# Batch normalisation with ReLU on one core: the first store split into two of one row per partition, and ScalarE's order fixed

**Chip, cores, metric.** One core of one Trainium2 chip. The metric is device time in microseconds (us); the kernel before takes 84.19 us (median of 3 runs, 84.05 to 84.41). The span that a profile shows is about 1.9 us shorter than the time of the same run (82.3 against 84.21).

## The reference

```python
# x: (32, 128, 32, 32) float32; gamma, beta, running_mean, running_var: (128,)
normalized = (x - running_mean[None, :, None, None]) / np.sqrt(running_var[None, :, None, None] + eps)
scaled = normalized * gamma[None, :, None, None] + beta[None, :, None, None]
return np.maximum(scaled, 0).astype(np.float32)
```

16.78 MB are read and 16.78 MB written, with one activation (ReLU of scale times x plus bias) between.

## The kernel before

x is seen as two tiles of 128 partitions with 16 rows of 1024 floats each; a row is one image of one channel, 4 KB, and a partition's 16 rows lie next to each other in HBM. The loads come in six pieces, the stores follow the same pieces.

```python
PIECES = (((0, 2), (2, 4), (4, 8), (8, 16)), ((0, 8), (8, 16)))
# ...
    for t in range(T):
        for a, b in PIECES[t]:
            xt = data.tile([P, b - a, HW], F32, name=f"x{t}_{a}")
            nc.sync.dma_start(out=xt, in_=xr[t, :, a:b, :])        # load queue (q1)
            tiles.append((t, a, b, xt))
# ... scale_t and bias_t are made from four small parameter loads on ScalarE's queue ...
    for t, a, b, xt in tiles:
        for j in range(a, b):
            nc.scalar.activation(out=xt[:, j - a, :], in_=xt[:, j - a, :], func=ACTF.Relu,
                                 bias=bias_t[:, j : j + 1], scale=scale_t[:, j : j + 1])
        nc.scalar.dma_start(out=outr[t, :, a:b, :], in_=xt)        # store queue (q10)
```

A scheduler may move a store behind activations of the next piece, and it did. Each of these transfers runs on all 16 DMA engines; what one partition has in a transfer is one packet, so an engine gets 8 packets of each: 8, 8, 16, 32, 32 and 32 KB long.

Of the kernel before, what the change touches and what calls it, by code (L numbers as in the profile page):

```python
# [1 line left out]

# [4 lines left out]


F32 = mybir.dt.float32
ACTF = mybir.ActivationFunctionType  # L10



J = 16

PIECES = (((0, 2), (2, 4), (4, 8), (8, 16)), ((0, 8), (8, 16)))


@with_exitstack
def kernel(  # L20
    ctx: ExitStack,
    tc: tile.TileContext,
    x: bass.AP,
    gamma: bass.AP,
    beta: bass.AP,
    running_mean: bass.AP,
    running_var: bass.AP,
    eps: bass.AP,
    out: bass.AP,
):  # L30
    nc = tc.nc
    B, C, H, W = x.shape
    HW = H * W
    P = nc.NUM_PARTITIONS
    assert C % J == 0 and P % (C // J) == 0 and (B * C) % (P * J) == 0
    Q = C // J
    T = B * C // (P * J)

    xr = x.rearrange("b c h w -> (b c) (h w)").rearrange("(t p j) w -> t p j w", p=P, j=J)
    outr = out.rearrange("b c h w -> (b c) (h w)").rearrange("(t p j) w -> t p j w", p=P, j=J)  # L40

    data = ctx.enter_context(tc.tile_pool(name="data", bufs=1))
    params = ctx.enter_context(tc.tile_pool(name="params", bufs=1))
    psum = ctx.enter_context(tc.tile_pool(name="psum", bufs=1, space=bass.MemoryType.PSUM))

    tiles = []
# [3 lines that stand above are left out]
            nc.sync.dma_start(out=xt, in_=xr[t, :, a:b, :])  # L50
            tiles.append((t, a, b, xt))



    raw = params.tile([Q, 4, J], F32, name="raw")
    for k, src in enumerate((running_var, gamma, running_mean, beta)):
        nc.scalar.dma_start(out=raw[:, k, :], in_=src.rearrange("(q j) -> q j", j=J))  # L57
    eps_t = params.tile([P, 1], F32, name="eps_t")
    nc.vector.memset(eps_t, float(eps))  # L59
    rep = params.tile([Q, P // Q, Q], F32, name="rep")  # L60
    nc.gpsimd.memset(rep, 1.0)  # L61
    nc.gpsimd.affine_select(  # L62
        out=rep,
        in_=rep,
        compare_op=mybir.AluOpType.is_equal,
        fill=0.0,
        base=0,
        pattern=[[0, P // Q], [-1, Q]],
        channel_multiplier=1,
    )  # L70
    cols = psum.tile([P, 4, J], F32, name="cols")
    nc.tensor.matmul(  # L72
        cols.rearrange("p k j -> p (k j)"),
        rep.rearrange("q r s -> q (r s)"),
        raw.rearrange("q k j -> q (k j)"),
        start=True,
        stop=True,
    )
    std_t = params.tile([P, J], F32, name="std_t")
    nc.scalar.activation(out=std_t, in_=cols[:, 0, :], func=ACTF.Sqrt, bias=eps_t[:, 0:1], scale=1.0)  # L80
    rstd_t = params.tile([P, J], F32, name="rstd_t")
    nc.vector.reciprocal(out=rstd_t, in_=std_t)  # L82
    scale_t = params.tile([P, J], F32, name="scale_t")
    nc.vector.tensor_mul(out=scale_t, in0=cols[:, 1, :], in1=rstd_t)  # L84
    ms_t = params.tile([P, J], F32, name="ms_t")
    nc.vector.tensor_mul(out=ms_t, in0=cols[:, 2, :], in1=scale_t)  # L86
    bias_t = params.tile([P, J], F32, name="bias_t")
    nc.vector.tensor_sub(out=bias_t, in0=cols[:, 3, :], in1=ms_t)  # L88

    for t, a, b, xt in tiles:  # L90
        for j in range(a, b):
            nc.scalar.activation(  # L92
                out=xt[:, j - a, :],
                in_=xt[:, j - a, :],
                func=ACTF.Relu,
                bias=bias_t[:, j : j + 1],
                scale=scale_t[:, j : j + 1],
            )
        nc.scalar.dma_start(out=outr[t, :, a:b, :], in_=xt)


# [1 line left out]
_INS = ['x', 'gamma', 'beta', 'running_mean', 'running_var', 'eps']  # L103
_OUTS = [((32, 128, 32, 32), 'float32')]

_NUMBERS = {'eps': 1e-05}


# [26 lines left out]
```

## Time and profile before

| | kernel before |
|---|---|
| time, span | 84.19 us, 82.3 us |
| busy share of the 16 DMA engines, load + store queue | 48.6 + 47.5 = 96.1% |
| busy share of ScalarE | 46% |
| last load landed, last store issued, last store landed | 51.2, 60.4, 81.4 us |

The DMA engines are full from 2 to 80 us, so time is the sum of what their packets take. The lines are in the prediction.

For this document I use one more reading. The trace has start and duration of each DMA packet. An undisturbed packet takes 309 ns for 8 KB, 611 for 16 KB and 1213 for 32 KB, and most take just that. **Slow time** here means, for one run, the sum over all packets of duration minus the undisturbed duration of that size, divided by 16 engines. In the kernel before it is 0.44 us in the first 6 us (the first packets of all) and 0.56 us after that, nearly all in 32 KB load packets; from the moment that loads are over it is zero.

### The profile page before, as it was taken

The numbers are of one execution on the slowest core, as the hardware profiler recorded it, in microseconds if no ns is written. First come the engines' busy times: TensorE is split into PE (matmuls) and PEld (weight loads), VectorE is DVE, ScalarE is ACT, GpSimd is POOL, SyncE is SP. The second block draws the span as 40 slices with busy tenths as digits, with TensorE's granted clock in tenths as the row PEclk, the third lists the DMA queues.
The fourth block names the chain that finished last, engine by engine and source line by source line (L and its number), as shares of the span: only waits on it lengthen the run. The fifth ranks groups of instructions, "written<-read, shape, count | busy, mean of one in ns | idle before, by whom it ended". The sixth has DMA issues, their size and how long they took to land.

```text
span 82.3 us, 117 instructions
## 1 busy us (share of the span) xinstructions
PE 0.7 (1%) x2; PEld 0.5 (1%) x2; DVE 0.8 (1%) x5; ACT 38.2 (46%) x34; POOL 0.8 (1%) x6
## 2 busy tenths in 40 slices
PE   0003000000000000000000000000000000000000
PEld 0002000000000000000000000000000000000000
DVE  0000300000000000000000000000000000000000
ACT  0600599990009999509999401999930000000000
POOL 3000000000000000000000000000000000000000
DMA  2899999997998997997999898997998999799790
GB/s 36 315 431 486 398 486 398 462 430 319 462 526 351 462 430 327 582 430 319 446 510 446 382 382 374 518 478 303 494 494 366 414 510 446 319 510 478 303 494 0
DMA packets 1792, 33.56 MB, mean 408 GB/s; under 512 B 256, under 2 KB 256, under 8 KB 256
## 3 DMA queue, kind: packets, MB, share of 16 engines
q1 hardware_dynamic: 864, 16.78, 48.6%
q10 hardware_dynamic: 928, 16.78, 47.5%
HBM read 16.78 MB, written 16.78 MB: 408 GB/s over the span
## 4 chain that ended last, share of the span: by engine, by line
DMA 60%; ACT 10%; ACTq 1%; issue 1%
DMA x<-in_x_dram 53%; ACT x L92 10%; DMA raw<-in_beta_dram 6%; ACTq L57 1%
## 5 line engine op out<-in xcount | busy, mean ns | idle before, releaser
L92 ACT ACTIVATE x<-x,bias_t,scale_t 128x1024 f32<-128x1024 f32 x32 | 36.6, 1227 | 15.4 <-DMA x<-in_x_dram 14.4
L80 ACT ACT_TABLE_LOAD x1 | 1.3, 1283 | 2.7 <-issue 2.7
L80 ACT ACTIVATE std_t<-cols,eps_t 128x16 f32<-128x16 f32 x1 | 0.3, 273 | 4.1 <-PE cols L72 4.1
L72 PE MATMUL cols<-raw,rep 8*128 8x64 f32 x2 | 0.7, 428 | 7.4 <-DMA raw<-in_beta_dram 7.4
L72 PEld LDWEIGHTS cols<-raw,rep 8*128 8x128 f32 x2 | 0.5, 306 | 7.4 <-issue 7.4
L62 POOL TENSOR_SCALAR_AFFINE_SELECT rep<-rep 8x128 f32<-8x128 f32 x1 | 0.4, 393 | 0.1
L82 DVE RECIPROCAL rstd_t<-std_t 128x16 f32<-128x16 f32 x1 | 0.3, 253 | 7.5 <-ACT std_t L80 7.5
L61 POOL MEMSET rep<- 8x128 f32 x1 | 0.2, 194 | 0.3 <-POOLq L116 0.3
L84 DVE TENSOR_TENSOR scale_t<-cols,rstd_t 128x16 f32<-128x16 f32 x1 | 0.2, 175 | 0.1
L86 DVE TENSOR_TENSOR ms_t<-cols,scale_t 128x16 f32<-128x16 f32 x1 | 0.2, 175 | 0.0
L88 DVE TENSOR_TENSOR bias_t<-cols,ms_t 128x16 f32<-128x16 f32 x1 | 0.2, 175 | 0.0
L116 POOL MEMSET const-bfloat16-1.0<- 128x1 bf16 x1 | 0.1, 106 | 0.0
L116 POOL MEMSET const-uint8-127<- 128x1 uint8 x1 | 0.1, 106 | 0.0
L116 POOL MEMSET const-float32-0.0<- 128x1 f32 x1 | 0.1, 103 | 0.3 <-issue 0.3
L116 POOL MEMSET const-float32-1.0<- 128x1 f32 x1 | 0.1, 103 | 0.0
L59 DVE MEMSET eps_t<- 128x1 f32 x1 | 0.1, 59 | 0.9 <-PEq L116 0.9
## 6 DMA issues: line engine op xcount, KB each, us to landing
x<-in_x_dram SPq DMA_DIRECT2D x3, 4096.0 KB, 22.7
out_dram<-x ACTq DMA_DIRECT2D x3, 4096.0 KB, 21.0
x<-in_x_dram SPq DMA_DIRECT2D x2, 1024.0 KB, 6.0
x<-in_x_dram SPq DMA_DIRECT2D x1, 2048.0 KB, 11.4
out_dram<-x ACTq DMA_DIRECT2D x2, 1024.0 KB, 25.9
out_dram<-x ACTq DMA_DIRECT2D x1, 2048.0 KB
raw<-in_running_var_dram ACTq DMA_DIRECT2D x1, 0.5 KB
raw<-in_gamma_dram ACTq DMA_DIRECT2D x1, 0.5 KB
```

Of the source, the lines that this page charges most:

```text
L57: nc.scalar.dma_start(out=raw[:, k, :], in_=src.rearrange("(q j) -> q j", j=J))
L59: nc.vector.memset(eps_t, float(eps))
L61: nc.gpsimd.memset(rep, 1.0)
L62: nc.gpsimd.affine_select(out=rep, in_=rep, compare_op=mybir.AluOpType.is_equal, fill=0.0, base=0, pattern=[[0, P // Q], [-1, Q]], channel ...
L72: nc.tensor.matmul(cols.rearrange("p k j -> p (k j)"), rep.rearrange("q r s -> q (r s)"), raw.rearrange("q k j -> q (k j)"), start=True, s ...
L80: nc.scalar.activation(out=std_t, in_=cols[:, 0, :], func=ACTF.Sqrt, bias=eps_t[:, 0:1], scale=1.0)
L82: nc.vector.reciprocal(out=rstd_t, in_=std_t)
L84: nc.vector.tensor_mul(out=scale_t, in0=cols[:, 1, :], in1=rstd_t)
L86: nc.vector.tensor_mul(out=ms_t, in0=cols[:, 2, :], in1=scale_t)
L88: nc.vector.tensor_sub(out=bias_t, in0=cols[:, 3, :], in1=ms_t)
L92: nc.scalar.activation(out=xt[:, j - a, :], in_=xt[:, j - a, :], func=ACTF.Relu, bias=bias_t[:, j : j + 1], scale=scale_t[:, j : j + 1],)
L116: nc = _bacc.Bacc("TRN2", target_bir_lowering=False, num_devices=1)
```

## The change

The intent is to get the first bytes out earlier, and to have each store issued as soon as its data are ready.

```diff
+STORE_CUTS = {(0, 1)}
...
-    for t, a, b, xt in tiles:
-        for j in range(a, b):
-            nc.scalar.activation(...)
-        nc.scalar.dma_start(out=outr[t, :, a:b, :], in_=xt)
+    with tc.manual_schedule(engines={mybir.EngineType.Activation}):
+        for t, a, b, xt in tiles:
+            first = a
+            for j in range(a, b):
+                nc.scalar.activation(...)          # unchanged
+                if j + 1 == b or (t, j + 1) in STORE_CUTS:
+                    nc.scalar.dma_start(
+                        out=outr[t, :, first : j + 1, :], in_=xt[:, first - a : j + 1 - a, :]
+                    )
+                    first = j + 1
```

More of the change, by code (lines that the diff above doesn't have):

```diff
@@ L88 @@
     nc.vector.tensor_sub(out=bias_t, in0=cols[:, 3, :], in1=ms_t)
-    for t, a, b, xt in tiles:
-        for j in range(a, b):
-            nc.scalar.activation(
-                out=xt[:, j - a, :],
-                in_=xt[:, j - a, :],
-                func=ACTF.Relu,
-                bias=bias_t[:, j : j + 1],
-                scale=scale_t[:, j : j + 1],
-            )
-        nc.scalar.dma_start(out=outr[t, :, a:b, :], in_=xt)
+    with tc.manual_schedule(engines={mybir.EngineType.Activation}):
+        for t, a, b, xt in tiles:
+            first = a
+            for j in range(a, b):
+                nc.scalar.activation(
+                    out=xt[:, j - a, :],
+                    in_=xt[:, j - a, :],
+                    func=ACTF.Relu,
+                    bias=bias_t[:, j : j + 1],
+                    scale=scale_t[:, j : j + 1],
+                )
+                if j + 1 == b or (t, j + 1) in STORE_CUTS:
+                    nc.scalar.dma_start(
+                        out=outr[t, :, first : j + 1, :], in_=xt[:, first - a : j + 1 - a, :]
+                    )
+                    first = j + 1
 _INS = ['x', 'gamma', 'beta', 'running_mean', 'running_var', 'eps']
```

## The prediction

> **What bounds the kernel now.** I read the page first (busy shares, then the forty slices), next the chain of waits, the ACT timeline, and last the DMA view in narrow windows, because the first two already say that this is a transfer problem.
>
> ```profile
> PE 0.7 (1%) x2; PEld 0.5 (1%) x2; DVE 0.8 (1%) x5; ACT 38.2 (46%) x34; POOL 0.8 (1%) x6
> ...
> ACT  0600599990009999509999401999930000000000
> ...
> DMA  2899999997998997997999898997998999799790
> ...
> q1 hardware_dynamic: 864, 16.78, 48.6%
> q10 hardware_dynamic: 928, 16.78, 47.5%
> ```
>
> The two queues together keep the 16 DMA engines busy for 48.6 + 47.5 = 96.1% of the 82.3 us span, 79.1 us. The DMA row has an 8 or more almost everywhere from the second slice (2.1 us) to the 39th (80.2 us); the 7s are slice edges, since the engines run in step on packets longer than half a slice. ScalarE, the only busy compute engine, is at 46%, and its row is blank for the last quarter. So there is no stretch in the middle in which a DMA engine waits for a store to be issued. The gaps are at the two ends only: about 1.8 us before the first load packet and about 1 us after the last store data.
>
> The chain of waits names a different thing and must be read with care:
>
> ```profile
> 7.27 43.91 DMA x<-in_x_dram
> ...
> 52.35 8.01 ACT x L92 x7
> ```
>
> It runs over the last load (landed at 51.2), seven activations, and ends with the issue of the last store at 60.4 us; the remaining 21.9 us are the stores. But that last store did not start to move when it was issued: it queued. The order of work on ScalarE shows how early each store is handed over:
>
> ```profile
> 9.38 3.50 ACT L92 ACTIVATE x<-x,bias_t,scale_t 128x1024 f32<-128x1024 f32 x3 [1.03 <-DVE bias_t L88]
> 11.78 0.38 ACTq L99 DMA_DIRECT2D out_dram<-x  x1
> ...
> 37.00 1.24 ACT L92 ACTIVATE x<-x,bias_t,scale_t 128x1024 f32<-128x1024 f32 x1 [2.97 <-DMA x<-in_x_dram]
> 37.00 0.34 ACTq L99 DMA_DIRECT2D out_dram<-x  x1
> ...
> 51.21 1.24 ACT L92 ACTIVATE x<-x,bias_t,scale_t 128x1024 f32<-128x1024 f32 x1 [5.05 <-DMA x<-in_x_dram]
> 51.21 0.34 ACTq L99 DMA_DIRECT2D out_dram<-x  x1
> ```
>
> Each store comes out one activation late. The one at 37.00 had its data ready at 34.0, that at 51.21 at 46.2, and both sat behind an activation of the next piece, which waited for its load. The change removes these delays of 3 and 5 us. Whether that is worth anything depends on whether the store queue was empty meanwhile, and it was not: stores of 1 + 1 + 2 MiB (4.19 MB) are issued by 18.9 us, and the DMA view summed over windows from 0 to 50 us has q10 moving only about 3.6 MB. In the trace the third store's last packets go at about 51.5 us, when the fourth has waited since 37 and the fifth has just been issued. From there stores run back to back: each 4 MiB store takes 9.7 us, with last packets at about 61.2, 70.9 and 80.6 us.
>
> Three windows, each holding data packets of one size, give the price of a packet (0.75 MB over 91 is 8 KB, 1.28 over 78 is 16 KB, 2.52 over 77 is 32 KB):
>
> ```profile
> q1 hardware_dynamic: 91, 0.75, 97.7%
> ...
> q1 hardware_dynamic: 78, 1.28, 99.3%
> ...
> q10 hardware_dynamic: 77, 2.52, 97.3%
> ```
>
> They are 2.8 to 4.6, 8 to 11 and 54 to 60 us. Share times 16 engines times length over packets: 0.977 x 16 x 1.8 / 91 = 309 ns for 8 KB; 0.993 x 16 x 3 / 78 = 611 ns for 16 KB; 0.973 x 16 x 6 / 77 = 1213 ns for 32 KB. One packet is what one partition has in one transfer, so each engine gets 8 packets of every transfer. Sum for one engine, loads and stores alike: 32 of 8 KB (9.89) + 16 of 16 KB (9.78) + 48 of 32 KB (58.22) = 77.9 us. Add the start at 1.8 us and roughly a microsecond of slower packets (the first sixteen or so after the start, and some 32 KB ones of 1.25 to 1.5 us), and the end of data at 80.5 to 81.1 us is accounted for. That sum bounds the kernel.
>
> **What the Trainium skill says.** "Perfetto Trace Analysis", section DMA Optimizations, recommends splitting DMAs with a condition: "If DMA engines are generally idle, splitting DMAs into smaller sections may allow the overall task to complete sooner." The condition does not hold here, at 96.1% busy. "DMA: Bandwidth & Descriptors", section Queues, rings and completion order, says that each DMA engine goes round its queues packet by packet. The trace agrees if a packet is what its record calls one: between 40 and 49 us both queues moved 80 packets, q1 2.62 MB of 32 KB ones and q10 1.31 MB of 16 KB ones. The same page, section Why small descriptors are slow (HBM only), says that each packet has a small fixed overhead. The trace agrees: 611 - 2 x (611 - 309) = 7 ns does not scale with size.
>
> **The change part by part.**
>
> Split of the first store: 128 packets of 8 KB become 256 of 4 KB, thus 16 an engine in place of 8. By the fit, one of 4 KB takes 309 - 302/2 = 158 ns, an estimate, as no 4 KB packet is in this trace. 16 x 158 - 8 x 309 = 2528 - 2472 = 56 ns. One more completion packet at 9 ns (the trace's 4-byte packets) makes 65 ns. This is on the path, because the engines are the path: +0.07 us.
>
> One more issue on ScalarE's queue, and no activation overlapping an issue: a store costs 0.34 to 0.38 us there and now stands in front of the next activation. The first activation ends at 10.62, so the first half goes out near 10.65 in place of 11.78; the next activation starts near 11.0 in place of 10.53. By the fourth store ScalarE is 1 to 2 us behind (about 20 us, before 18.6), then waits for the load of the next piece anyway (24.9). Off the path: 0.
>
> Fixed order: the 4 MiB stores are issued when their data are ready. They join a queue with a backlog: 0 at the end.
>
> Earlier and smaller store packets change the interleaving. Beside loads of 32 KB, a round on one engine was 1213 + 309 ns for the first two stores (16 rounds). For the first it becomes 1213 + 158, with twice as many rounds. While the loads last, stores get less, so the loads finish earlier. They overlapped 8 + 8 store packets of 8 KB and 8 of 16 KB (9.8 us an engine); now they overlap 16 of 4 KB and about 8 of 8 KB (5.0 us). The last load should land about 4 to 5 us earlier, near 46 to 47 us, and the last store be issued near 56. What the loads gain the stores lose; bytes and engines are the same: 0.
>
> Semaphores: the program assigns its transfers to eight completion semaphores in turn, and one more store among them shifts the rest. In the built code the fourth load now waits for the first parameter load (landed at 2.2, and that load was issued at 2.17), the fifth for the third parameter load (about 6.6, formerly the second, 6.0), and the sixth for the landing of the second data load (8.2, formerly the fourth parameter load, 7.26). So the diff leaves the loads alone and the build does not. But the fourth load's data move from 12.1 us, the fifth's from 24 and the sixth's from 36: 0.
>
> Sum: 84.19 + 0.07 = 84.26 us, rounded to 84.25.
>
> **The rivals.**
>
> (a) The earlier first store fills idle DMA time. For it: it goes out 1.1 us earlier, and one could count on 1.1 us. Against it: at 10.7 us the engines are loading at 99.3%. It would give 83.1; even this is within 2%.
>
> (b) The delayed 4 MiB stores were holding the end back, and 3 or 5 us come off (79 to 81 us). For it: the chain of waits has ScalarE's last part on it. Against it: the backlog, and 9.7 us per 4 MiB store with no hole from 51 to 80 us.
>
> (c) A new wait bites. The store of the second tile's first half shares a semaphore with the first half-store and cannot be issued before that has landed. I put that landing near 26 us and the issue near 44: harmless, unless half-stores drain far slower. The last store has still more room: it must be in the queue when the one before it is done, at about 70 us, and comes near 56.
>
> (d) 4 KB packets are much worse than the fit. Rows written then lie 64 KB apart in HBM, as they do now with 8 KB packets at full price. If one took 309 ns, it would be 16 x 151 = 2.4 us more, 86.6 us: the one plausible way to slower by over 2%.
>
> **Range and chances.** The working gives +0.07 us. The three runs of before span 0.36 us, and slower packets (about 1 us an engine in sum) may fall otherwise with another interleaving, by perhaps 0.3 us either way. Hence 83.8 to 84.8. Faster by over 2% needs 1.7 us, more than all idle time that a store could fill: 1%. Slower by over 2% needs (d) or something like it: 2%. Within 2%: 97%.
>
> **What would show it right or wrong.** Right: both queues' shares again sum to about 96%; 4 KB packets near 158 ns; last load landing at 46 to 48 us; first store issue near 10.7; the 4 MiB stores issued at once after their eighth activation; last store issue near 56 and its landing still near 81.5 us. Wrong: an end that moves along with the last store's issue (b); slices below 7 in the DMA row between 51 and 80 us (c); store packets of 4 KB well over 158 ns (d); a first store that shortens the sum of packet times.

## The result, and the profile after

The changed kernel takes 83.78 us (median of 6 runs, 83.72 to 83.92) against 84.18 of the kernel before in the same rounds (6 runs, 84.05 to 84.41). The ratio is 0.9953, 95% interval 0.9937 to 0.9969. Ratios in this document are the mean time of one kernel's fast runs over the mean of the other's of the same rounds, so not quite the ratio of the medians. By the 2% rule this is "the same", as forecast, but 83.78 lies just below my range of 83.8 to 84.8, and I had expected 0.07 us more where there were 0.4 less.

First the lines of the changed kernel's page that answer to those of before: the DMA row (tenths of busy share in forty slices) and the two queues (packets, MB, share of 16 engines' span).

```profile
DMA  2899999989899999979789798996999899799690
...
q1 hardware_dynamic: 864, 16.78, 48.4%
q10 hardware_dynamic: 1072, 16.78, 47.8%
```

The row is as full as it was, so no idle time was filled. The shares have the answer, once they are turned into microseconds: q1 had 48.6% of 82.3 us, 40.0 us an engine, and has 48.4% of 81.9, 39.6; q10 had 39.1 and has 39.1. **The same load packets, which the change does not touch, take 0.4 us less.** From the packet records, which are not rounded to a tenth of a per cent: q1 39.99 to 39.63, q10 39.04 to 39.12 us.

ScalarE's timeline (start, us, engine, line, what; "ACTq" is the issue of a transfer) shows the mechanics of the change:

```profile
10.99 0.38 ACTq L104 DMA_DIRECT2D out_dram<-x  x1
...
33.05 0.34 ACTq L104 DMA_DIRECT2D out_dram<-x  x1
...
44.00 0.34 ACTq L104 DMA_DIRECT2D out_dram<-x  x1
46.79 9.16 ACT L96 ACTIVATE x<-x,bias_t,scale_t 128x1024 f32<-128x1024 f32 x8 [2.82 <-DMA x<-in_x_dram]
55.97 0.34 ACTq L104 DMA_DIRECT2D out_dram<-x  x1
```

First store issued at 10.99 (forecast 10.7), the 4 MiB stores right after their eighth activation, last load landed at 46.8 (46 to 47), last store issued at 55.97 (56). The end did not follow: the last store's issue came 4.4 us earlier, the span shrank by 0.4.

The price of a 4 KB packet is read as in the prediction, from a window of 26 to 33 us in which q10 moves nothing else:

```profile
q10 hardware_dynamic: 81, 0.33, 11.5%
```

0.115 x 16 x 7 / 81 = 159 ns; my estimate was 158. So the part that I had priced came out (q10 +0.08 us against +0.07), and something I had not priced came on top.

Where are the slow packets? Two windows of q1, each holding exactly the 16 load packets (one an engine) in flight as the store queue begins to move. A window counts a packet whole if it starts in it, so shares go over 100%. The first is the kernel before, 14.45 to 15.15 us, the second the changed kernel, 12.9 to 13.8 us.

```profile
q1 hardware_dynamic: 16, 0.52, 197.6%
```

```profile
q1 hardware_dynamic: 16, 0.52, 138.5%
```

1.976 x 0.7 = 1383 ns and 1.385 x 0.9 = 1247 ns a packet, where 1213 is undisturbed. That is one round (one packet an engine) of about 22 that run beside stores; the rest of the difference is spread over several. The same round in the repeats c1 (kernel before, 14.3 to 15.2 us) and c2 (changed kernel, 12.9 to 13.8 us), both on chip 5:

```profile
q1 hardware_dynamic: 16, 0.52, 168.2%
```

```profile
q1 hardware_dynamic: 16, 0.52, 148.8%
```

That is 1514 and 1339 ns: both are higher there, and the order is the same.

### The profile page after: what moved, and what is told of

Same layout as the page of the kernel before. It is cut to its first block, busy times and chain, and to the rows that moved or that the text cites. A ratio compares the mean times of both kernels' runs of the same rounds, so it can differ in the third digit from the quotient of the medians.

```text
span 81.9 us, 119 instructions
## 1 busy us (share of the span) xinstructions
PE 0.7 (1%) x2; PEld 0.5 (1%) x2; DVE 0.8 (1%) x5; ACT 38.5 (47%) x34; POOL 0.8 (1%) x6
## 3 DMA queue, kind: packets, MB, share of 16 engines
q1 hardware_dynamic: 864, 16.78, 48.4%
## 4 chain that ended last, share of the span: by engine, by line
DMA 56%; ACT 11%; SPq 0%; issue 0%
DMA x<-in_x_dram 56%; ACT x L96 11%; SPq L52 0%
```

## The experiments

All were correct, all timed runs fast; the two repeats c1 and c2 are single runs, whose state is unknown. Times before were 84.14 to 84.28 us in all jobs. The diffs are against the changed kernel if nothing else is said, and they are shortened. The three theories: **O**, the fixed order and the earlier stores gained the 0.4 us; **S**, smaller store packets beside the loads make fewer slow load packets (a revision, after e3 and e4, of theory M, by which it was fewer store bytes beside the loads); **N**, the shifted semaphores and thus the loads' issue did it.

| run | first store's packets | time us | ratio to before | slow time 6-25 us | after 25 us | load queue, sum |
|---|---|---|---|---|---|---|
| before | 8 KB | 84.18 | | 0.38 | 0.18 | 39.99 |
| c1 (before again) | 8 | 84.26 | | 0.63 | 0.25 | 40.18 |
| e1 order only | 8 | 84.27 | 1.0008 | 0.39 | 0.44 | 40.21 |
| e6 two halves by partitions | 8 | 84.06 | 0.9987 | 0.66 | 0.20 | 40.21 |
| e7 second store split | 8 | 83.91 | 0.9963 | 0.61 | 0.02 | 39.89 |
| after | 4 | 83.78 | 0.9953 | 0.13 | 0.06 | 39.63 |
| c2, c3 (after again) | 4 | 83.91, 83.91 | c3 0.9957 | 0.36, 0.39 | 0.05, 0.17 | 39.75, 39.90 |
| e2 split only | 4 | 83.83 | 0.9960 | 0.16 | 0.10 | 39.80 |
| e5 order and split, other place | 4 | 83.83 | 0.9958 | 0.16 | 0.06 | 39.66 |
| e15 second row first | 4 | 84.01 | 0.9971 | 0.17 | 0.49 | 40.15 |
| e8 four rows in one store | 16 | 84.58 | 1.0040 | 1.01 | 0.00 | 40.39 |
| e9 four stores of half a row | 2 | 84.93 | 1.0085 | 0.06 | 0.94 | 40.42 |

(Slow time and sums come from one profiled run each. Half-widths of the ratios' intervals are 0.0012 to 0.0022.)

### e1: only the order

```diff
-STORE_CUTS = {(0, 1)}
+STORE_CUTS = set()
```

> Only ScalarE's order is fixed, the first store stays whole (8 KB packets); waits of the loads are those of the kernel before. Theory M (the gain of 0.4 us comes from fewer slow 32 KB load packets, because less store traffic runs beside the loads): as many store bytes run beside the loads as before (about 9.8 us an engine), so slow packets sum to about 0.5 us an engine after 6 us, time 84.1 to 84.3, ratio 0.998 to 1.002. Theory O (the gain comes from stores handed over when ready): 83.8, ratio 0.995, last store issued near 58 us.

84.27 us, ratio 1.0008 (0.9994 to 1.0022). The stores of 4 MiB were issued at 34.16 and 46.37 us, as soon as their data were there, and nothing came of it. Its queues on the page:

```profile
q1 hardware_dynamic: 864, 16.78, 48.8%
q10 hardware_dynamic: 928, 16.78, 47.4%
```

48.8% of 82.4 us is 40.2 us for the loads, none of the gain. Theory O falls.

### e2: only the split

```diff
-    with tc.manual_schedule(engines={mybir.EngineType.Activation}):
+    if True:
```

> Only the store is split; the scheduler puts both halves after the second activation, so neither is early, and the 4 MiB stores are again one activation late. Theory M: 83.7 to 83.9, ratio about 0.9955, slow packets after 6 us about 0.2 us an engine, last load landing near 47. Theory O, or a theory that the early first half matters: 84.2, ratio 1.000.

83.83 us, 0.9960 (0.9945 to 0.9974): the whole gain, though the 4 MiB stores are late again (34.85 and 47.03 us). One thing was not as I had said: in the trace the first half is issued at 10.91 us, after the first activation. The position in ScalarE's program is behind the second activation, but the issue waits for the first one's end only and runs beside the second. So e2 parts the split from the order, not small packets from an early start.

### e3: stores held back, and e4: small packets throughout

e3 holds the stores of tile 0 back until a row of the second tile's first piece, then issues them whole:

```diff
+                if (t, j) == (1, HOLD):       # HOLD = 3; then issue all stores held so far
+                    for ht, ha, hb, hx in held:
+                        nc.scalar.dma_start(out=outr[ht, :, ha:hb, :], in_=hx)
```

> Stores whole, but all held back until four rows of the second tile's first piece are done (near 37 us), so that they run beside at most the last one or two load packets. Theory M: no slow load packet after 6 us (sum near 0), DMA row without holes, 83.5 to 83.7, ratio 0.992 to 0.994. Theory O: 84.2 or more. If the stores come too late for the engines, a hole near 41 us and more time than M says.

84.60 us, 1.0047. The hold did less than was meant: the four stores were issued at 32.65 to 34.03 us, as the first rows of that piece began, and not near 37, since here too the issue did not wait for the activations in front of it; about five load rounds were then mixed with stores, not one or two. Theory M (slow time goes with the store bytes that run beside loads) is wrong all the same: with only those five rounds, against about 22 in the kernel before, the slow time was 0.98 us an engine. It has two lumps: 0.37 us at 35 to 37.5 us, where the stores begin to move, and 0.47 us in the very last load packets, at 41.3 to 42.1 us. So the slow packets are not spread evenly over the mixing, they cluster where it begins and, here, where it ends.

e4 cuts the second and third store to single rows too:

```diff
-STORE_CUTS = {(0, 1)}
+STORE_CUTS = {(0, j) for j in range(1, 8)}
```

> As the changed kernel, but the second and third store are also cut to one row per partition. Packet overhead: 16 x 159 - 8 x 309 = 72 ns for the second, 32 x 159 - 8 x 611 = 200 ns for the third, 5 more completions 45 ns: +0.3 us. Theory M: 24 packets of 4 KB (3.8 us an engine) run beside loads in place of 5.0 us, slow packets 0.1 to 0.2 us, so 83.9 to 84.1 in all, ratio 0.997 to 0.999. A theory that 4 KB packets are themselves the cheaper ones: 83.6 or less.

85.68 us, 1.0179, far off what any theory said. ScalarE's timeline shows stores that themselves wait for stores:

```profile
25.28 0.34 ACTq L104 DMA_DIRECT2D out_dram<-x  x1
25.67 1.24 ACT L96 ACTIVATE x<-x,bias_t,scale_t 128x1024 f32<-128x1024 f32 x1 [4.95 <-DMA out_dram<-x]
```

The transfers take eight completion semaphores in turn; with five more stores a late one shares its semaphore with an early one and waits until that has landed. The sixth load was caught as well: it was issued at 35.85 us, right after the landing of the second row store (35.84), while the packets of the load before it ended at 34.7 to 35.1 us; its first data packet moved at 39.6. The row for 34 to 41 us (forty slices of 0.175 us; in the zeros at its start, packets that began before 34 us still ran) shows stores alone keeping the engines busy, and weaker slices as the load queue returns:

```profile
DMA  0000489999999999999999999896799999910409
```

0.85 us of slow time lie in the last two load packets before the queue ran dry, 0.55 us where loads come back (0.44 of it in store packets). This is the rival (c) of my prediction, in a kernel where it does bite; not by idle engines, though: of the 1.65 us that the span is longer than before, 1.36 are packet time (queue sums 80.38 against 79.03 us).

### e6, e7 and the repeats: more transfers, another store, chance

e6 has two stores, both after the second activation, cut by partitions, so packets stay 8 KB:

```diff
+                if (t, j) == (0, 1):
+                    for i in (0, 64):
+                        nc.scalar.dma_start(out=outr[t, i : i + 64, a:b, :], in_=xt[i : i + 64, :, :])
```

> The first store is again two stores, both after the second activation as in e2, but cut by partitions (64 and 64), so the packets stay 8 KB and each engine still gets 8 of them; the loads five and six wait as in the changed kernel. Theory S (smaller store packets beside the loads make fewer slow load packets): no gain, 84.1 to 84.3, ratio 0.999 to 1.002, slow packets after 6 us 0.5 to 0.9 us an engine as in the kernel before and e1. Rival theory N (one more transfer shifts the semaphores and thus the issue of the loads, and that is the gain): 83.8, ratio 0.996.

84.06 us, 0.9987 (0.9973 to 1.0002), slow time 0.86 us. The loads five and six wait as in the changed kernel, and the gain is not there. Theory N falls.

e7 splits the second store, not the first (`STORE_CUTS = {(0, 3)}`).

> The second store is cut to one row instead of the first. In the profiles so far the slow packets between 13 and 24 us, where stores begin beside loads, sum to 0.36 to 0.39 us an engine with 8 KB store packets (before, e1) and to 0.14 to 0.17 with 4 KB (after, e2); later ones to 0.18 to 0.44 against 0.06 to 0.10. Theory S by stretch: the first part stays at about 0.37, the later part falls to about 0.1, packets +0.07: 83.9 to 84.1, ratio 0.997 to 0.999. If only the start of the mixing counts: 84.2 to 84.3. If only the earlier end of the loads counts: 83.8.

83.91 us, 0.9963 (0.9949 to 0.9977). By stretch it is as theory S said: 0.61 us while the 8 KB packets of the first store begin, then 0.02. In all it has 0.63 us after 6 us, against 0.89 (c1) and 0.86 (e6) in the profiles with 8 KB that were taken on the same chip: 0.25 us less, where the time gained 0.31.

> The kernel before once more, for a second profile: slow load packets after 6 us again 0.5 to 0.8 us an engine if the difference between the two kernels is steady, anything down to 0.2 if it was chance.

> The changed kernel once more, for a second profile: slow load packets after 6 us again 0.15 to 0.3 us an engine if the difference is steady.

They show how much: the kernel before had 0.89 us after 6 us in its second profile (0.56 in the first), the changed one 0.42 (0.19), and 0.55 in a third (c3). The groups differ, but their edges almost touch, and c2 and c3 are above what was expected of them.

Part of that scatter goes with the chip, as a comparison made afterwards shows. c1, c2, e6 and e7 ran on chip 5, and c3, e12 and e13 on chip 7. On these two the slow time from 6 to 25 us is 0.61 to 0.66 us with 8 KB first and 0.36 to 0.39 with 4 KB; in the other runs that begin to store before 25 us it is 0.38 to 0.39 and 0.13 to 0.24. (For the kernels before and after the chip is not recorded; their numbers put them with the others.) The step from 8 to 4 KB is about 0.25 us in either group.

### e8 and e9: the dose

e8 puts the first two load pieces into one tile and stores its four rows at once, in 16 KB packets; e9 stores each of the first two rows as two half rows, in 2 KB packets.

```diff
+    first_four = data.tile([P, 4, HW], F32, name="x0_0")     # e8; two loads into it as before
+                if (t, j) == (0, 3):
+                    nc.scalar.dma_start(out=outr[t, :, 0:4, :], in_=first_four)
```

```diff
+                if (t, a) == (0, 0):                           # e9
+                    for h in (0, HW // 2):
+                        nc.scalar.dma_start(out=outr[t, :, j : j + 1, h : h + HW // 2],
+                                            in_=xt[:, j : j + 1, h : h + HW // 2])
```

> Dose up: the first two load pieces lie in one tile (loads as before, two transfers), and their four rows leave as one store of 16 KB packets; ScalarE's order fixed. Packets: 8 x 611 in place of 16 x 309, -0.06 us. The four profiles with 8 KB first (before, its repeat, e1, e6) have slow packets of 0.56, 0.89, 0.83, 0.86 us an engine after 6 us, the three with 4 KB first (after, its repeat, e2) 0.19, 0.42, 0.26. Theory S: more than with 8 KB, about 1.0 to 1.5, last load landing near 54, time 84.3 to 84.9, ratio 1.002 to 1.008. If packet size of the store is not the cause: 84.1, ratio 0.999.

> Dose down: the first store is four stores of half a row, 2 KB packets. Packets: 32 of about 83 ns (an estimate from the fit) in place of 16 x 159, +0.12 us, and two more completions, +0.02. Theory S: slow packets after 6 us 0.1 to 0.25 us an engine, time 83.7 to 83.9, ratio 0.994 to 0.997, with the last load landing near 43 to 44; no longer a gain over the changed kernel. The sixth load waits for the first 2 KB store (landing near 25 us), before its data are needed: no hole. If it waits longer, the load queue runs dry as in e4 and it is over 84.2.

e8: 84.58 us, 1.0040 (1.0020 to 1.0060), slow time 1.01 us, all of it before 25 us. The 16 load packets that start between 17 and 18 us, just ahead of its first store packets:

```profile
q1 hardware_dynamic: 16, 0.52, 164.0%
```

1640 ns each. With 2, 4, 8 and 16 KB the slow time where stores begin (6 to 25 us) is 0.06, 0.13 to 0.39, 0.38 to 0.66 and 1.01 us. That is a dose and its effect. Clearer still is the one round in flight as the first store packets come up, averaged in every profile with the store beginning beside loads: 1217 to 1242 ns with 2 KB (four profiles), 1225 to 1339 with 4 KB (nine), 1383 to 1529 with 8 KB (six), 1640 with 16 KB (one). Between 4 and 8 KB nothing overlaps, whatever the chip; 2 and 4 KB do.

e9: 84.93 us, 1.0085, missed. Where stores begin it did as expected (0.06 us), and its loads were done early, but the last two load packets of every engine were slow. Window 40.4 to 42.6 us:

```profile
q1 hardware_dynamic: 32, 1.05, 151.7%
q10 hardware_dynamic: 31, 0.06, 7.4%
```

1.517 x 16 x 2.2 / 32 = 1669 ns a packet. What was saved at the start is lost here and more.

### e10 to e14: attempts to keep both ends

e10 stores row 0 as two half rows and row 1 whole; e11 is the changed kernel with `STORE_CUTS = {(0, 1), (0, 3)}`.

> An attempt to beat both: row 0 leaves as two stores of 2 KB packets, row 1 as one of 4 KB. Packets: 16 x 84 + 8 x 159 = 2616 in place of 2544 ns, +0.07 us over the changed kernel, one more completion 0.01. Where stores begin (6 to 25 us) theory S expects slow packets of 0.06 us an engine as in e9 in place of 0.13 to 0.36. At the end of the loads two 4 KB packets and the eight of 8 KB of the second store are left behind the last load, in e9 ten of 2 KB and those eight. If the slow last loads of e9 came from small packets left behind them, they shrink: 83.6 to 83.8, ratio 0.993 to 0.995. If they came from a whole 8 KB store still waiting, they stay near 0.9: 84.5 to 84.9.

> The changed kernel with the second store cut to one row too. Packets +0.07, completion +0.01 over the changed kernel; slow packets where stores begin 0.13 to 0.36 as there. At the end of the loads ten packets of 4 KB are left behind the last load (in the changed kernel three of 8 KB, in e7 five of 4 KB, neither with slow last loads). If many small packets behind the last loads slow them, as e9 and e3 suggest: 0.4 to 0.9 more, 84.3 to 84.7. If not: 83.8 to 83.9.

e10 took 84.70 us (1.0057), e11 84.53 us (1.0037). Slow time from 6 to 25 us is 0.07 and 0.18 us, as the dose says; in the last load packets it is 0.92 and 0.70 us. From these I made a rule, that ten or more small packets left behind the last load slow it. e12 and e13 were to test it: rows 2 to 7 in one tile and one store of 24 KB packets, ahead of it row 0 in 2 KB packets and row 1 in 4 KB (e12) or 2 KB (e13).

> Row 0 in two stores of 2 KB packets, row 1 in one of 4 KB, rows 2 to 7 in one store of 24 KB packets (their two loads unchanged, into one tile). Behind the last load two 4 KB packets and then 24 KB ones are left. Slow packets after 6 us: where stores begin 0.06 as in e9 and e10, at the end of the loads about 0 if the rule of few small packets left behind holds, so 0.1 in all against 0.19 to 0.42 in the changed kernel; packets 1344 + 1272 + 7296 = 9.91 us against 9.90 there. Time 83.5 to 83.75, 0.1 to 0.2 us under the changed kernel. If the rule is wrong: slow last loads again, 84.5 or more.

> As e12, but row 1 too in two stores of 2 KB packets: ten packets of 2 KB, 20 KB in all, are left behind the last load. If the number of small packets left behind counts: slow last loads of 0.5 to 0.9 us an engine, 84.2 to 84.7. If their bytes count (20 to 24 KB were harmless in e7 and after): 83.6 to 83.8.

> The changed kernel again, timed in the same rounds as e12 and e13: 83.7 to 83.95, ratio 0.994 to 0.997, slow packets after 6 us 0.15 to 0.45 us an engine.

e12: 84.50 us (1.0023), with 0.17 us from 6 to 25 us (0.06 expected) and 0.90 us in the last load packets, although only two or three small packets stood behind them. The rule falls. e13: 84.70 us (1.0041), 1.23 us there. c3, the changed kernel in the same rounds: 83.91 us (0.9957, 0.9937 to 0.9977). e14 has the changed kernel's two 4 KB stores and then the 24 KB one:

> Changed kernel's first store (4 KB, first half early), then rows 2 to 7 as one store of 24 KB packets, so the last six load rounds run beside 24 KB packets and the loads end near 49 to 50 us. Where stores begin as in the changed kernel 0.13 to 0.39. If the slow last loads belong to loads that end early (below 46 us so far): none here, and 83.7 to 84.0. If they belong to a large change of packet size behind small ones, as 4 to 24 KB in e12: 0.5 or more, 84.2 to 84.6.

84.15 us (1.0013, 0.9986 to 1.0040). Its last load packets were not slow, but the one ahead of the first 24 KB store packet was, on all engines (window 35.4 to 35.9 us):

```profile
q1 hardware_dynamic: 16, 0.52, 346.7%
```

3.467 x 0.5 = 1734 ns. So a change to larger store packets costs in mid-stream too, not only at the first store.

### e5 and e15: small packets or an early start

In e1 to e14 the runs with a smaller first store packet also began to store earlier. e5 was to part this: both halves after the second activation.

```diff
+                if (t, j) == (0, 1):
+                    for i in range(2):
+                        nc.scalar.dma_start(out=outr[t, :, i : i + 1, :], in_=xt[:, i : i + 1, :])
```

> First store as two of 4 KB packets, both after the second activation (issued near 11.7 and 12.1 us), so that stores begin to move near 16.0 us as in the kernel before. If the packet size counts: slow packets 6 to 25 us 0.13 to 0.39 us an engine, 83.75 to 83.95, ratio 0.995 to 0.997. If the early start was what counted: 0.38 to 0.66 and 84.1 to 84.3, ratio 0.999 to 1.002.

83.83 us, 0.9958, but it did not part them: the first half went out after the first activation again, as in e2.

```profile
9.50 2.37 ACT L94 ACTIVATE x<-x,bias_t,scale_t 128x1024 f32<-128x1024 f32 x2 [1.02 <-DVE bias_t L89]
10.77 1.50 ACTq L103 DMA_DIRECT2D out_dram<-x  x2
```

e15 sends row 1 first (`for i in (1, 0)`), so that both must wait. Its waits are those of e6, and only the packet size differs.

> As e5, but row 1 goes out before row 0, so both stores really have to wait for the second activation; semaphore waits are those of e6, whose two stores have 8 KB packets, and only the packet size differs from e6. The first store packet should move near 16.0 us, as in the kernel before and e6. If the packet size counts: slow packets 6 to 25 us 0.1 to 0.39 us an engine, in all 0.2 to 0.55, 83.75 to 83.95, ratio 0.995 to 0.997. If the early first half was what counted: 0.38 to 0.66, in all 0.56 to 0.89, 84.05 to 84.3, ratio 0.998 to 1.002.

```profile
9.48 2.37 ACT L94 ACTIVATE x<-x,bias_t,scale_t 128x1024 f32<-128x1024 f32 x2 [1.02 <-DVE bias_t L89]
11.88 0.86 ACTq L103 DMA_DIRECT2D out_dram<-x  x2
```

Stores now begin to move at 15.8 us, as in the kernel before (16.0), and the slow time from 6 to 25 us is 0.17 us, against 0.66 in e6. The load packets ahead of the first store packet (14.3 to 15.2 us):

```profile
q1 hardware_dynamic: 16, 0.52, 139.3%
```

1.393 x 0.9 = 1254 ns, as in the changed kernel. So where stores begin it is the packet size, not the moment. (e15 and e6 ran on different chips, and no 8 KB profile of e15's chip exists; but 0.17 us and 1254 ns lie below every 8 KB profile of any chip, 0.38 us and 1383 ns at the least.) In time e15 keeps part of the gain: 84.01 us, 0.9971 (0.9956 to 0.9987), between my two forecasts, and its profile has 0.30 us of slow time in the last load packets, which the changed kernel has not. With these its slow time is 0.66 us in all, above the 0.2 to 0.55 expected for packet size; e15 settles the place where stores begin, and not the whole gain.

## Why the prediction was wrong

**Right, step by step.** The bound (full DMA engines, sum of packet times), the 4 KB packet (158 forecast, 159 ns measured), the store queue's +0.07 us (+0.08), the times of issue and of the last load's landing, the shifted semaphore waits of the loads (issued at 6.98 and 7.99 us, forecast 6.6 and 8.2) and their harmlessness, and the verdict on the fixed order: nothing (e1). Rivals (a), (b) and (d) did not come true; (c) did only in other kernels (e4, and in e9 one 4 MiB store issued 2.4 us late, at 34.97 us).

**Read wrongly, without effect on the sum.** "Each store comes out one activation late" holds for the fourth and fifth store. The first three were issued as their own last activation ended (the first at 11.78 us, beside the third activation); e2 and e5, which began early against my expectation, are the same case. And I let eight 16 KB store packets run beside the loads; the trace has six, so stores took 8.6 us an engine there, not 9.8, and 4.7 in the changed kernel, not 5.0.

**Wrong: one term of the sum.** The prediction says of the interleaving: "What the loads gain the stores lose; bytes and engines are the same: 0." And of the slow packets, that they "may fall otherwise with another interleaving, by perhaps 0.3 us either way". I had seen them, had put them into the account of the kernel before ("roughly a microsecond of slower packets"), and then took their change to be chance with mean zero. It is not: of the prediction's own signs of being wrong, the last one came, "a first store that shortens the sum of packet times", and the last store landed at 81.0 us, not near 81.5. Over the profiles with 8 KB packets first and nothing else cut (before, c1, e1, e6) against those with 4 KB first, early, and nothing else cut (after, c2, c3, e2, e5), in us an engine:

| mean of profiles | 8 KB first | 4 KB first | difference |
|---|---|---|---|
| slow time after 6 us | 0.79 | 0.33 | -0.46 |
| slow time in the first 6 us | 0.36 | 0.42 | +0.06 |
| load queue, sum | 40.15 | 39.75 | -0.40 |
| store queue, sum | 39.04 | 39.12 | +0.08 |
| last engine's end minus the mean of the 16 | 0.34 | 0.23 | -0.11 |
| span | 82.39 | 81.99 | -0.40 |

-0.40 + 0.08 - 0.11 = -0.43, near the span's -0.40; the rest is small changes in idle time and after the last packet. So the term that I set to 0 is about -0.46 (the same on chip 5 alone, and without chips 5 and 7). A further -0.11 comes from engines that end closer together, which I had not thought of, but there the single profiles overlap (0.26 to 0.46 against 0.17 to 0.31). Of the -0.46, 0.28 us lie between 6 and 25 us, where stores begin, and 0.18 later. The range was missed by only 0.02 us; the term was missed by all of its size.

**Shown and not shown.** Shown: the gain is in the load packets' durations; the split brings it and the order does not; where stores begin, the slow time goes with the size of the store packets (2 to 16 KB), and not with the moment (e15) or the number of transfers (e6). Not shown: why a load packet is slowed by larger store packets behind it, and what makes the later 0.18 us. (In the kernel before, 16 KB store packets begin at 40.4 us beside loads that last to 50.2; in the changed one they begin at 46.4, after the last load packet at 46.1. No run tested this alone.) Open, too: why the last one or two load packets are slow in e3, e9 to e13 and a little in e15, and hardly or not at all (0.11 us at most) in the kernel before, the changed one, e2, e5, e7, e8 and e14. My rule for it failed in e12. Thus the gain of the changed kernel also rests on that not happening there, and I cannot say which other cut would be safe. None of fifteen variants was faster than the changed kernel beyond the scatter; e2 and e5 are as fast.

## What to carry to other kernels

When the DMA engines are full, splitting or hurrying a store cannot fill idle time, and an estimate from bytes and packet counts was right to about half a per cent for this change, but 1 to 2% too low in e9 and e4; what remains is how loads and stores disturb one another, and that can be read from the packets' durations, queue by queue. A queue that the change leaves alone may still change its own time: turn both queues' shares into microseconds before and after. And count the transfers before cutting further: here the ninth and later ones wait for semaphores of earlier ones, and with five more stores (e4) late waits, packet overhead and slow packets came to 1.8%.

## What the Trainium skill lacked or had wrong

- "DMA: Bandwidth & Descriptors", Queues, rings and completion order: has the turn-taking between queues, which the traces agree with, but nothing on one queue's packets being slowed by the other's. Here a 32 KB load packet of 1213 ns took on average 1225 to 1339, 1383 to 1529 and 1640 ns in the round where 4, 8 and 16 KB store packets began to follow.
- Same page and section: it measures a packet by its descriptors, about 9 to 17 of them, and not by bytes or time. In these traces the queues alternate by packets of one partition's contiguous bytes, from 2 to 32 KB, and 32 KB take 1213 ns; how many descriptors such a packet has, no trace shows.
- "Perfetto Trace Analysis", DMA Optimizations: names generally idle DMA engines as the case in which splitting helps. Here a split paid 0.4 us (0.5%) at 96% busy, through the load packets' durations and not through idle time; other splits cost up to 1.8% (e4).
- No page has how long a store waits behind the other queue on busy engines: issued at 11.78 us in the kernel before, its first packet moved at 16.0 us; the first load of the program, on idle engines, was issued at 0.81 and moved at 1.81 us.
